# Hybrid layer step on Trainium2, SSD stage: the last places of groups 0 and 1 run behind the next group's first units; PSUM banks 4, 1, 3 instead of 3, 2, 3

## Chip, cores and metric

The kernel runs on one core of one Trainium2 chip. The metric is the device time of one execution in microseconds (us), the median of several runs.

## What is computed

One decoder layer with three parallel branches on 512 prompt rows and 64 sample rows (8 sequences of 8 new rows each). Only branch B, the Mamba-2 SSD, is touched. Cut to it, the reference is:

```
proj = rmsnorm(x) @ w_in                      # z, xBC, dt are slices of proj
xbc  = silu(causal_conv(xBC, conv_state))     # 4 taps; the last 3 rows of xBC are returned as the new conv state
xs, B, C = split(xbc);  dt = softplus(dt + dt_bias);  a = -exp(a_log)
# per group of 4 heads, in 4 chunks of 128 prompt rows; h is 64 x 128 for each head
y_diag = (C B^T * decay) (dt x)               # within a chunk
state  = B^T (wdec dt x);  h = dec*h + state  # from chunk to chunk
y_off  = (C h_prev) * exp(a_cs)               # from the chunks before
y = y_diag + y_off + d_skip*x;  y = rmsnorm_group(y * silu(z)) * g;  h_b = y
out += sigmoid(merge) * (h_b @ w_proj_b)
```

The sample rows go the same way as one chunk of 8 rows for each sequence, with a start state h0 of each sequence that is loaded from memory (8 x 32 heads x 64 x 128), read by C and rewritten.

## The kernel before

**Stages.** The span's first 651 us are the SSD stage; the other branches and the output projection follow and are not touched. There are 8 groups g. Activations lie in on-chip memory with channels across the 128 partitions and 576 rows (512 prompt, 64 sample) in the free direction, in two halves of 288.

**Units.** The stage's projections are a list of jobs, and each job has two halves; a half is called a unit here. A unit is 24 products of 128x128 by 128x288 into one PSUM bank (`gemm_half`, L167; each weight is taken as a high and a low part, and so is the activation, which makes three products for each of 8 blocks). A job's `load` fetches weights (L130, on SyncE), its `prep` splits them (`whi` on ScalarE L98, `wlo` on VectorE L99), its `half` runs the unit and evicts it. Job kinds: `conv_job(g, ci)` for the x, B and C columns of a group with the convolution behind it (evicted on ScalarE L412/L416, taps on VectorE L426, result L430/L437), `z_job` (evicted by tanh L470 on ScalarE and L471 on VectorE), `proj_job` (two times 12 products in each unit, added into `m_sb` by VectorE L763) and `gate_job`. While group g is worked on, the convolutions of group g+1 run.

**Places.** Between the units stands the small work of the SSD recurrence. `steps(g)` lists it as twelve places, and a table (`PLACES`) says behind which unit of the group each place comes. TensorE's order is just the order in which this program is written (`tc.manual_schedule` for TensorE alone); the order on VectorE, ScalarE, GpSimd and SyncE comes from a scheduler. The steps that matter below:

- `chunk_a(g, c)`: three transposes into an `sps` bank (L511), from which VectorE makes `xdt` and `xdd` (L514, L517) and ScalarE `BT` (L519); then `chunk_cb` forms C B^T (L540) and VectorE multiplies the decays `e` with it (L541).
- `decays(g, c)`: loads `e` by a DMA on SyncE's queue (L496), adds the mask (VectorE L497), exponentials (ScalarE L499). There are three buffers for `e`.
- `yd`: products into a `yps` bank (L556) and their addition to `ysb` (VectorE L567). `yd(g, 4)` is that of the sample rows; `c_h0` (L682, evicted by ScalarE L686) also uses `yps`.
- `state` (L575, first chunk evicted by ScalarE L579), `state_out` (L588/L590), `y_off` (L600/L603), `y_smp` (L613), `gate_y` (L693 to L695), `norm_y` (L707 to L713).
- `h0_T`: transposes of the sample's start states (L652, evicted by ScalarE L654); `h0_new`: the new states (L661, scaled on ScalarE L666, added on VectorE L667).
- `conv_out(g)`: a transpose (L446) into an `sps` bank, a copy (ScalarE L448), and eight DMAs that ScalarE issues (L451, L452).

**Banks.** The eight PSUM banks are dealt out as three pools, L67: `acc` for the units, `yps` and `sps` for the small work. Each pool goes round its banks, and a new use waits until the bank's last one has been read: with three `sps` banks the fourth small step in a row waits for the first one's readers.

Of the kernel before, what the change touches and what calls it, by code (L numbers as in the profile page):

```python
# [14 lines left out]
PSUM = bass.MemoryType.PSUM  # L15
# [27 lines left out]
def tile_hybrid_step(  # L43
# [20 lines left out]
    bank = {}  # L64

    def banks(stack, acc, y, s):

        for k, n in (("acc", acc), ("yps", y), ("sps", s)):
            bank[k] = stack.enter_context(tc.tile_pool(name=f"ps_{k}{acc}", bufs=n, space=PSUM, reuse_waits="tile"))

    def acc_tile():
        return bank["acc"].tile([P, 512], F32, tag="acc", name="acc")
# [113 lines left out]
    xl = lambda k: hn_lo[:, k]  # L186

    with ExitStack() as stb:
        banks(stb, 3, 2, 3)
        ws["pool"] = stb.enter_context(tc.tile_pool(name="wb", bufs=2))  # L190
        pb = stb.enter_context(tc.tile_pool(name="pb", bufs=1))
        xbuf = mpool.tile([P, KD * T], F32, tag="m", name="xbuf")
# [26 lines left out]
        for tiles in ((0, 1, 2), (3, 4)):  # L219
            n = len(tiles)  # L220
# [11 lines left out]
            w = 3 * P if n == 3 else P + TS  # L232
            for k in range(KD):
# [4 lines left out]
                g = gcol[:, k:k + 1]  # L238
# [408 lines left out]
        def h0_T(g, j, f):  # L647

            d = st_[g]
            tp = s_tile()  # L650
            for b in range(4):
                PE.transpose(tp[:, b * P:(b + 1) * P], d["h0", j][:, 4 * f + b], ident)  # L652
            h0T = pb.tile([P, 4 * P], F32, tag="h0T", name="h0T", bufs=2)
            d["h0T", j, f] = h0T, S.copy(h0T, tp)  # L654

        def h0_new(g, j, f):

            d = st_[g]
            xst, btd = d["st", f]
            sps = s_tile()  # L660
            PE.matmul(sps, lhsT=xst[:, 2 * j:2 * j + 2].rearrange("p h d -> p (h d)"),  # L661
                      rhs=btd.rearrange("p b n -> p (b n)"), start=True, stop=True)
            h4 = d["h0", j][:, 4 * f:4 * f + 4]
            dl = d["ebc"][:, j, TP + 32 * f:TP + 32 * f + 32].rearrange("p (b t) -> p b t", t=LS)[:, :, LS - 1:LS]
            for b in range(4):
                S.activation(h4[:, b], h4[:, b], AF.Copy, scale=dl[:, b])  # L666
            V.tensor_tensor(h4, h4, sps.rearrange("p (b n) -> p b n", b=4), ALU.add)  # L667
            if f == 1:
                hd = 4 * g + 2 * j
                S.dma_start(out=ssm_s[0, :, hd:hd + 2].rearrange("b r d n -> (r d) b n"), in_=d["h0", j])  # L670
# [72 lines left out]
        def proj_job(r, p):  # L743

            k = {}

            def load():
                if p % 2 == 0:
                    gate_th["p", r, p // 2] = load_block(w_proj_b[0], r * 512, 4, [(p * 256, 512)])

            def prep():
                k["w"] = wsplit(gate_th["p", r, p // 2], 4, (p % 2) * 256, 256)

            def half(j):
                jj = 2 * p + j
                w = [t[:, :, j * P:(j + 1) * P] for t in k["w"]]
                for f in range(2):
                    ps, sl = gemm_half(w, 4, lambda i: hb[4 * r + i][:, 0], lambda i: hb[4 * r + i][:, 1], f)
                    dst = m_sb[:, jj, sl]
                    if r == 0:  # L760
                        S.copy(dst, ps)
                    else:
                        V.tensor_tensor(dst, dst, ps, ALU.add)  # L763
                    if r == 3:
                        V.scalar_tensor_tensor(dst, gate_th[jj][:, sl], 1.0, dst, ALU.add, ALU.mult)
                if r == 3:
                    S.dma_start(out=m_scr[:, jj], in_=m_sb[:, jj])
            return Job(load, prep, half)


        with tc.manual_schedule(engines={mybir.EngineType.PE}):
            def group_jobs(g):

                c = [conv_job(g + 1, ci) for ci in range(4)] if g + 1 < G else [gate_job(0), gate_job(1), gate_job(2), gate_job(3)]
                z = [z_job(g, 0), z_job(g, 1)]
                if g == 0:
                    return [z[0], *c, z[1]]
                if g == 1:
                    return [c[0], c[1], z[0], c[2], c[3], z[1]]
                p = [proj_job(g // 2 - 1, 2 * (g % 2) + i) for i in range(2)]  # L780
                a, b = (p, z) if g % 2 else (z, p)
                return [c[0], a[0], c[1], a[1], c[2], b[0], c[3], b[1]]

            def yd(g, *cs):
                y_add(g, cs, y_diag(g, cs))

            def steps(g):

                w = [[] for _ in range(12)]
                w[0] = [lambda: start_y(g), lambda: decays(g, 2), lambda: chunk_a(g, 1)]  # L790
                w[1] = [lambda: state(g, 0)]
                if g > 0:
                    w[1] += [lambda: y_smp(g - 1), lambda: gate_y(g - 1)]
                w[2] = [lambda: state(g, 1), lambda: chunk_a(g, 2)]
                w[3] = [lambda: y_off(g, 1), lambda: yd(g, 0, 1), lambda: decays(g, 3)]
                if g > 0:
                    w[3] += [lambda: norm_y(g - 1)]
                w[4] = [lambda: state(g, 2), lambda: chunk_a(g, 3), lambda: decays(g, 4)]
                w[5] = [lambda: y_off(g, 2), lambda: chunk_a(g, 4), lambda: h0_load(g, 0)]
                w[6] = [lambda: state(g, 3), lambda: chunk_t4(g), lambda: h0_load(g, 1)]  # L800
                w[7] = [lambda: y_off(g, 3), lambda: chunk_cb(g, 4)]
                w[8] = [lambda: yd(g, 2, 3), lambda: state_out(g), lambda: h0_T(g, 0, 0)]
                w[9] = [lambda: h0_T(g, 0, 1), lambda: h0_new(g, 0, 0), lambda: h0_new(g, 0, 1)]
                w[10] = [lambda: c_h0(g, 0), lambda: h0_T(g, 1, 0), lambda: h0_T(g, 1, 1)]
                w[11] = [lambda: h0_new(g, 1, 0), lambda: h0_new(g, 1, 1), lambda: c_h0(g, 1), lambda: yd(g, 4)]
                return w

            halves = [(j, h) for j in (conv_job(0, ci) for ci in range(4)) for h in range(2)]  # L810
            between = {}

            def put(u, *fs):
                between.setdefault(u, []).extend(fs)

            put(7, lambda: decays(0, 0), lambda: decays(0, 1))
            PLACES = {0: (2, 3, 4, 5, 6, 7, 8, 9, 10, 11, 12, 13), 1: (1, 3, 4, 5, 6, 7, 8, 9, 10, 11, 12, 13)}
            for g in range(G):
                u0 = len(halves)
                halves += [(j, h) for j in group_jobs(g) for h in range(2)]  # L820
                n = len(halves) - u0
                if g == 0:
                    put(u0 + 1, lambda: chunk_a(0, 0), lambda: conv_out(0))
                else:

                    between[u0 - 1] = between.get(u0 - 1, []) + [lambda g=g: chunk_a(g, 0)]
                w = steps(g)
                at = PLACES.get(g, (1, 2, 3, 5, 6, 7, 8, 9, 11, 12, 13, 14) if g == 2 else (0, 1, 2, 4, 5, 7, 8, 9, 10, 12, 13, 14))
                for i, a in enumerate(at):
                    put(u0 + a, *w[i])  # L830
                if g + 1 < G:
                    put(u0 + n - 3, lambda g=g: decays(g + 1, 0), lambda g=g: decays(g + 1, 1))
                    put(u0 + n - 1, lambda g=g: conv_out(g + 1))
            units = []
            for u, x in enumerate(halves):
                units += [x, (None, between.get(u, []))]
            tail = {0: [lambda: y_smp(G - 1), lambda: gate_y(G - 1)], 5: [lambda: norm_y(G - 1)]}
            for i, u in enumerate([(j, h) for j in (gate_job(jj) for jj in range(4, 8)) for h in range(2)]):
                units += [u, (None, tail.get(i, []))]
            units += [(j, h) for j in (proj_job(3, p) for p in range(4)) for h in range(2)]  # L840

            jobs = [u[0] for u in units if u[0] is not None and u[1] == 0]
            at = {id(j): i for i, j in enumerate(jobs)}
            jobs[0].load()
            jobs[0].prep()
            jobs[1].load()
            for j, h in units:
                if j is None:
                    for w_ in h:
                        w_()  # L850
                    continue
                i = at[id(j)]
                if h == 0:
                    if i + 2 < len(jobs):
                        jobs[i + 2].load()
                    if i + 1 < len(jobs):
                        jobs[i + 1].prep()
                j.half(h)
# [587 lines left out]
    for i in range(4):  # L1446
# [17 lines left out]
        n = len(pieces)  # L1464
# [44 lines left out]
```

## Time and profile before

| | |
|---|---|
| median of 3 runs | 1154.28 us (1149.95 to 1155.85) |
| profiled execution, its own time | 1156.32 us |
| span of the profiled execution | 1154.6 us, mean granted TensorE clock 0.985 |
| TensorE matmuls (PE) | 1106.8 us busy, 96% |
| VectorE (DVE) | 780.2 us busy, 68% |
| ScalarE (ACT) | 619.9 us busy, 54% |
| GpSimd (POOL) | 28.4 us busy, 2% |
| chain of work that ended last | PE 89%, DVE 4%, DMA 3%, ACT 2%, issue 1% |

PE is the TensorE matmul, PEld its weight load, SP is SyncE; ACTq and SPq are the sequencers that issue DMAs. Busy means that at least one instruction runs. The granted clock is a share of the full 2.4 GHz: 1.00 is 2.4 GHz, 0.50 is 1.2 GHz, and a value between them is a stretch that was partly at one and partly at the other. A row of the timeline gives start, duration, the instruction, and in brackets how long the engine had been idle before it and what released it.

### The profile page before, as it was taken

The numbers are of one execution on the slowest core, as the hardware profiler recorded it, in microseconds if no ns is written. First come the engines' busy times: TensorE is split into PE (matmuls) and PEld (weight loads), VectorE is DVE, ScalarE is ACT, GpSimd is POOL, SyncE is SP. The second block draws the span as 40 slices with busy tenths as digits, with TensorE's granted clock in tenths as the row PEclk, the third lists the DMA queues.
The fourth block names the chain that finished last, engine by engine and source line by source line (L and its number), as shares of the span: only waits on it lengthen the run. The fifth ranks groups of instructions, "written<-read, shape, count | busy, mean of one in ns | idle before, by whom it ended". The sixth has DMA issues, their size and how long they took to land.

```text
span 1154.6 us, 20412 instructions
## 1 busy us (share of the span) xinstructions
PE 1106.8 (96%) x8200; PEld 1030.4 (89%) x8200; DVE 780.2 (68%) x1444; ACT 619.9 (54%) x1291; POOL 28.4 (2%) x109
## 2 busy tenths in 40 slices
PE   5999898999999989999999999999999999999997
PEld 3989887899999989999999877899999999889776
DVE  5778495867788686687634654786975567775743
ACT  6457576676767667565554244343653236564521
POOL 1010000000000000000000000000000000000000
PEclk9999898999999999999999999999999999999999
DMA  6433433445253534525242525631363353465411
GB/s 171 121 88 111 122 107 89 126 142 146 84 154 97 151 92 132 146 71 168 66 145 95 189 73 165 192 110 39 109 209 113 118 185 105 121 183 195 152 47 73
DMA packets 160334, 144.38 MB, mean 125 GB/s; under 512 B 10152, under 2 KB 141264, under 8 KB 160240
## 3 DMA queue, kind: packets, MB, share of 16 engines
q1 hardware_dynamic: 137136, 125.60, 35.5%
q10 hardware_dynamic: 23104, 17.49, 4.8%
q8 instruction: 64, 1.05, 0.4%
q14 instruction: 30, 0.25, 0.1%
HBM read 123.61 MB, written 19.46 MB: 124 GB/s over the span
## 4 chain that ended last, share of the span: by engine, by line
PE 89%; DVE 4%; DMA 3%; ACT 2%; issue 1%; SPq 0%; ACTq 0%; DVEq 0%
PE acc L167 37%; PE acc L923 15%; PE acc L154 12%; PE acc L1053 4%; PE acc L1458 4%; DMA e<-a_scr 2%; PE acc L1118 2%; PE yps L556 2%; PE sps L652 1%; PE sps L511 1%; PE sps L575 1%; DVE cacc L426 1%; PE sps L600 1%; PE yps L682 1%; PE sps L540 1%
## 5 line engine op out<-in xcount | busy, mean ns | idle before, releaser
L167 PE MATMUL acc<-hn_hi,whi 128*128 128x288 f32 x896 | 275.4, 307 | 2.0 <-ACT thm L740 0.8
L167 PE MATMUL acc<-hn_hi,wlo 128*128 128x288 f32 x896 | 269.0, 300 | 2.6 <-DVE wlo L99 2.6
L167 PE MATMUL acc<-hn_lo,whi 128*128 128x288 f32 x896 | 269.0, 300 | 0.0
L167 PEld LDWEIGHTS acc<-hn_hi,whi 128*128 128x128 f32 x896 | 173.1, 193 | 3.5 <-ACT thm L740 1.0
L167 PEld LDWEIGHTS acc<-hn_hi,wlo 128*128 128x128 f32 x896 | 172.6, 193 | 3.1 <-DVE wlo L99 3.1
L167 PEld LDWEIGHTS acc<-hn_lo,whi 128*128 128x128 f32 x896 | 173.0, 193 | 0.3
L98 ACT CAST w<-wraw 128x1024 fp32r<-128x1024 f32 (+1 forms) x64 | 59.2, 942 | 103.4 <-PE acc L923 24.0
L167 PE MATMUL acc<-hb,whi 128*128 128x288 f32 x512 | 105.2, 301 | 4.5 <-DVE m_sb L763 4.5
L99 DVE TENSOR_TENSOR wlo<-wraw,whi 128x1024 fp32r<-128x1024 f32 x72 | 87.9, 1220 | 28.9 <-ACT whi L98 28.7
L98 ACT CAST whi<-wraw 128x1024 fp32r<-128x1024 f32 x72 | 75.6, 1050 | 46.1 <-PE acc L167 43.9
L99 DVE TENSOR_TENSOR w<-wraw,w 128x1024 fp32r<-128x1024 f32 x64 | 68.5, 1087 | 36.3 <-ACT w L98 36.0
L923 PE MATMUL acc<-hn_hi,w 128*128 128x288 f32 x512 | 89.5, 300 | 0.0
L167 PEld LDWEIGHTS acc<-hb,whi 128*128 128x128 f32 x512 | 82.0, 189 | 5.2 <-DVE m_sb L763 5.0
L923 PE MATMUL acc<-tT,w 128*128 128x288 f32 x576 | 85.9, 298 | 0.0
L426 DVE SCALAR_TENSOR_TENSOR cacc<-raw,cwh,cacc 128x600 f32<-128x600 f32 x96 | 80.5, 839 | 7.3 <-ACT cacc L424 6.6
L923 PEld LDWEIGHTS acc<-tT,w 128*128 128x128 f32 x576 | 78.4, 188 | 0.9 <-issue 0.9
L923 PEld LDWEIGHTS acc<-hn_hi,w 128*128 128x128 f32 x512 | 74.1, 188 | 2.1 <-DVE thx L941 0.5
L167 PE MATMUL acc<-hb,wlo 128*128 128x288 f32 x256 | 75.7, 296 | 0.0
L99 DVE TENSOR_TENSOR w<-S,w 128x1024 fp32r<-128x1024 f32 x32 | 39.2, 1224 | 25.0 <-ACT w L98 25.0
L499 ACT ACTIVATE e<-e,nacs 128x128 f32<-128x128 f32 (+1 forms) x160 | 49.7, 381 | 8.7 <-DVE e L497 8.7
L154 PE MATMUL acc<-ha,w 128*128 128x288 f32 x384 | 51.6, 295 | 0.0
L154 PE MATMUL acc<-hn_hi,w 128*128 128x288 f32 x256 | 51.2, 295 | 0.0
(393 smaller groups left out, 2122.5 us busy)
## 6 DMA issues: line engine op xcount, KB each, us to landing
wraw<-in_w_in_dram SPq DMA_DIRECT2D x44, 1024.0 KB
wraw<-in_w_in_dram SPq DMA_DIRECT2D x16, 512.0 KB
e<-a_scr SPq DMA_DIRECT2D x32, 256.0 KB
h<-in_state_ssm_dram SPq DMA_DIRECT2D x16, 512.0 KB
out_dram<-h ACTq DMA_DIRECT2D x16, 512.0 KB
wraw<-in_w_proj_b_dram SPq DMA_DIRECT2D x8, 1024.0 KB
ebc<-e_scr SPq DMA_DIRECT2D x16, 288.0 KB
wraw<-in_w_mem_kv_dram SPq DMA_DIRECT2D x4, 1024.0 KB
```

What stands on the lines that cost most here:

```text
L98: S.copy(hi, v)
L99: (e or V).tensor_tensor(lo, v, hi, ALU.subtract)
L154: PE.matmul(ps[:n, :width], lhsT=a, rhs=b[:, sl], start=(i == 0), stop=(i == last))
L167: PE.matmul(ps[:, 0:HT], lhsT=a[:, k], rhs=b(k)[:, sl], start=(n == 0), stop=(n == 3 * nk - 1))
L426: V.scalar_tensor_tensor(a[:, 0:n], raw[:, i:i + n], cwh[:, i, q:q + 1], a[:, 0:n], ALU.mult, ALU.add)
L499: S.activation(e[:, h, 0:w], e[:, h, 0:w], AF.Exp, bias=nacs[:, c, h0_ + h:h0_ + h + 1])
L511: PE.transpose(tp[:, j * P:(j + 1) * P], xs[:, j, c0:c0 + P], ident)
L556: m = PE.matmul(y4[64 * r:64 * r + 64, i, j], lhsT=xdt[:, h], rhs=e[:, h, 0:w], start=True, stop=True)
L923: PE.matmul(ps[:, 0:HT], lhsT=w[:, r, k], rhs=x(q, k), start=first and n == 0, stop=n == 11, skip_group_check=True)
L1053: PE.matmul(pss[i], lhsT=x(k)[:, c], rhs=w[:, r, k2], start=(k + q == 0), stop=(k == KD - 1 and q == 2))
L1118: PE.matmul(pss[i], lhsT=x[xr], rhs=w[:, r, k2], start=(k + q == 0), stop=(k == KD - 1 and q == 2))
L1458: PE.matmul(ps[:, 0:cn], lhsT=x(k)[:, c], rhs=w, start=(k + q == 0), stop=(k == KD - 1 and q == 2))
```

## The change

Five edits, all in the order of the SSD stage or in its banks. The number of instructions on each engine stays as it is.

1. Banks: `acc` 4, `yps` 1, `sps` 3 instead of 3, 2, 3 (the pool's name is made from another number so that it stays unique).
2. Group 0's places come one unit later, so that its last one falls behind the third unit of group 1; group 1's last three places come one unit later. `chunk_a(0, 0)` and `conv_out(0)` too come one unit later; `chunk_a(1, 0)` and `chunk_a(2, 0)` stay behind the last unit of the group before.
3. Group 2's jobs stand in another order (c0 c1 z0 z1 c2 p0 c3 p1 instead of c0 z0 c1 z1 c2 p0 c3 p1), and its places follow the table that group 1 had before.
4. `yd(g, 4)`, the sample's in-chunk products, moves in all groups from the end of the last place (w[11], behind `c_h0(g, 1)`) to the start of place 9 (w[9]), two places earlier.
5. `conv_out(1)` and `conv_out(2)` move from the last unit of the group before to a place behind the fourth unit of their own group, ahead of `state(g, 0)`, `y_smp` and `gate_y` there. The others stay.

```diff
-            bank[k] = stack.enter_context(tc.tile_pool(name=f"ps_{k}{acc}", bufs=n, space=PSUM, reuse_waits="tile"))
+            bank[k] = stack.enter_context(tc.tile_pool(name=f"ps_{k}{y}", bufs=n, space=PSUM, reuse_waits="tile"))
...
-        banks(stb, 3, 2, 3)
+        banks(stb, 4, 1, 3)
...
+                if g == 2:
+                    return [c[0], c[1], z[0], z[1], c[2], proj_job(0, 0), c[3], proj_job(0, 1)]
...
-                w[9] = [lambda: h0_T(g, 0, 1), lambda: h0_new(g, 0, 0), lambda: h0_new(g, 0, 1)]
+                w[9] = [lambda: yd(g, 4), lambda: h0_T(g, 0, 1), lambda: h0_new(g, 0, 0), lambda: h0_new(g, 0, 1)]
                 w[10] = [lambda: c_h0(g, 0), lambda: h0_T(g, 1, 0), lambda: h0_T(g, 1, 1)]
-                w[11] = [lambda: h0_new(g, 1, 0), lambda: h0_new(g, 1, 1), lambda: c_h0(g, 1), lambda: yd(g, 4)]
+                w[11] = [lambda: h0_new(g, 1, 0), lambda: h0_new(g, 1, 1), lambda: c_h0(g, 1)]
...
-            PLACES = {0: (2, 3, 4, 5, 6, 7, 8, 9, 10, 11, 12, 13), 1: (1, 3, 4, 5, 6, 7, 8, 9, 10, 11, 12, 13)}
+            PLACES = {0: (3, 4, 5, 6, 7, 8, 9, 10, 11, 12, 13, 14), 1: (1, 3, 4, 5, 6, 7, 8, 9, 10, 12, 13, 14),
+                      2: (1, 3, 4, 5, 6, 7, 8, 9, 10, 11, 12, 13)}
...
-                    put(u0 + 1, lambda: chunk_a(0, 0), lambda: conv_out(0))
+                    put(u0 + 2, lambda: chunk_a(0, 0), lambda: conv_out(0))
...
-                    put(u0 + n - 1, lambda g=g: conv_out(g + 1))
+                    put(u0 + n + (3 if g < 2 else -1), lambda g=g: conv_out(g + 1))
```

**TensorE, where group 0 ends and group 1 begins.** `sps` and `yps` are tiles of those pools, `h` the start states, `xs`, `B` and `C` the convolved columns; "x4" counts instructions. Before, in a row:

```order
L652 MATMUL sps<-ident,h_1194 128x128 x4
L661 MATMUL sps<-btd,xst 128x512 x2
L446 MATMUL sps<-ident,cg 108x128
L511 MATMUL sps<-ident,xs 128x128 x3
L540 MATMUL sps<-C,xs 128x128
```

These five steps take six `sps` banks one after the other with no unit between them. With the change, in a row:

```order
L556 MATMUL yps<-e,xdt 64x128 x8
L588 MATMUL sps<-ident,hT 128x128 x2
L652 MATMUL sps<-ident,h_1229 128x128 x4
L511 MATMUL sps<-ident,xs 128x128 x3
L540 MATMUL sps<-C,xs 128x128
```

The first steps of the next group (L511, L540) now follow the end of `yd` and the first `h0_T` (L652), one unit ahead of the second `h0_T`, and the two L661 and `conv_out`'s L446 have gone to later units.

**ScalarE, in the first units of group 1**, around the copy of the first chunk's state, L579. Before:

```order
L98 CAST whi<-wraw 128x1024
L416 COPY raw<-acc 128x224
L417 COPY raw<-acc 128x8x8
L579 COPY hT<-sps 128x256
L424 ACTIVATE cacc<-raw,cbh,cwh 128x600
L470 ACTIVATE th<-acc 128x288
L694 ACTIVATE zs<-ysb 128x1152
```

With the change:

```order
L452 DMA out_dram<-co 24x128
L428 ACTIVATE raw<-cacc 128x600
L451 DMA out_dram<-co 3x128
L452 DMA out_dram<-co 24x128
L579 COPY hT<-sps 128x256
L694 ACTIVATE zs<-ysb 128x1152
L470 ACTIVATE th<-acc 128x288
```

The last of the eight DMA issues of `conv_out` now stand ahead of L579 on ScalarE, and so does the tanh of the convolution (L428).

**VectorE, at the end of group 3**, where only `yd(3, 4)` has moved; L567 with 128x2x64 is its addition, and L497 the masks of the next group's decays. Before:

```order
L99 TENSOR_TENSOR wlo<-wraw,whi 128x1024
L667 TENSOR_TENSOR h_3547<-h_3547,sps 128x512 x2
L420 COPY cg<-raw 128x3
L421 COPY cg<-raw 128x24
L426 SCALAR_TENSOR_TENSOR cacc<-raw,cwh,cacc 128x600 x3
L99 TENSOR_TENSOR wlo<-wraw,whi 128x1024
L430 SCALAR_TENSOR_TENSOR C<-raw,cacc 128x512
L434 SCALAR_TENSOR_TENSOR C<-raw,cacc 128x64
L471 SCALAR_TENSOR_TENSOR zs<-th,acc 128x288
L667 TENSOR_TENSOR h_3604<-h_3604,sps 128x512 x2
L567 TENSOR_TENSOR ysb<-ysb,yps 128x2x64
L497 TENSOR_TENSOR e<-e,tri 128x512
```

With the change:

```order
L497 TENSOR_TENSOR e<-e,tri 128x512 x2
L471 SCALAR_TENSOR_TENSOR zs<-th,acc 128x288
L99 TENSOR_TENSOR wlo<-wraw,whi 128x1024
L567 TENSOR_TENSOR ysb<-ysb,yps 128x2x64
L667 TENSOR_TENSOR h_3547<-h_3547,sps 128x512 x2
L420 COPY cg<-raw 128x3
L421 COPY cg<-raw 128x24
L497 TENSOR_TENSOR e<-e,tri 128x512
L426 SCALAR_TENSOR_TENSOR cacc<-raw,cwh,cacc 128x600 x3
```

The addition L567 now stands ahead of the first two L667, and the third mask L497 ahead of the convolution's taps L426.

## Rows read from the trace of the kernel before

**Rows 1.** Busy time by stretch. Columns: the stretch in us from the span's start, its length, busy us (and count) of PE, PEld, DVE, ACT and POOL, the granted TensorE clock, the DMA engines' busy share, GB/s.

```profile
71.00:77.00 6.00, 6.00 (x36) 6.00 (x36) 1.46 (x4) 0.67 (x2) 0.25 (x2) 0.72 0.70 184
...
116.00:124.00 8.00, 6.72 (x29) 6.35 (x30) 4.22 (x7) 3.48 (x10) 0.00 (x0) 0.57 0.43 119
...
133.00:138.00 5.00, 5.00 (x27) 5.00 (x28) 5.00 (x9) 2.71 (x7) 0.68 (x1) 0.66 0.39 114
...
181.00:189.00 8.00, 7.27 (x34) 6.55 (x37) 3.08 (x5) 2.98 (x9) 0.00 (x0) 0.57 0.28 76
...
198.00:203.00 5.00, 5.00 (x27) 4.92 (x26) 4.95 (x9) 2.56 (x8) 1.06 (x1) 0.66 0.37 105
...
260.00:405.00 145.00, 144.25 (x1174) 139.56 (x1174) 111.23 (x218) 99.50 (x236) 4.24 (x22) 1.00 0.44 127
...
426.00:431.00 5.00, 4.27 (x21) 4.27 (x22) 4.51 (x11) 3.59 (x8) 0.48 (x3) 0.66 0.01 2
```

**Rows 2.** The timeline of PE: the matmuls from 67 to 430 us before which it had waited (one of 0.75 at 359.01 stands in rows 7), with what released them.

```profile
70.80 0.49 PE L540 MATMUL sps<-C,xs 128*128 128x128 f32 x2 [2.58 <-DVE C L430]
...
116.71 0.46 PE L446 MATMUL sps<-ident,cg 128*108 128x128 f32 x1 [2.39 <-ACT h0T L654]
...
117.73 0.90 PE L511 MATMUL sps<-ident,xs 128*128 128x128 f32 x3 [0.57 <-DVE h L667]
...
132.96 0.46 PE L540 MATMUL sps<-C,xs 128*128 128x128 f32 x2 [1.96 <-DVE h L667]
...
152.56 0.40 PE L167 MATMUL acc<-hn_hi,whi 128*128 128x288 f32 x1 [0.76 <-DVE zs L471]
...
161.67 0.52 PE L511 MATMUL sps<-ident,xs 128*128 128x128 f32 x3 [0.80 <-ACT BT L519]
...
180.84 0.32 PE L446 MATMUL sps<-ident,cg 128*108 128x128 f32 x1 [1.78 <-DVE h L667]
...
181.47 0.90 PE L511 MATMUL sps<-ident,xs 128*128 128x128 f32 x3 [0.30 <-ACT h0T L654]
...
182.80 0.79 PE L540 MATMUL sps<-C,xs 128*128 128x128 f32 x2 [0.43 <-ACT co L448]
...
197.59 0.46 PE L540 MATMUL sps<-C,xs 128*128 128x128 f32 x2 [1.96 <-DVE h L667]
...
211.45 0.40 PE L167 MATMUL acc<-hn_hi,whi 128*128 128x288 f32 x1 [0.49 <-ACT raw L412]
...
226.92 0.52 PE L511 MATMUL sps<-ident,xs 128*128 128x128 f32 x3 [1.91 <-issue]
...
407.82 0.53 PE L167 MATMUL acc<-hb,whi 128*128 128x288 f32 x2 [1.78 <-DVE m_sb L763]
...
426.73 0.53 PE L167 MATMUL acc<-hb,whi 128*128 128x288 f32 x2 [2.76 <-DVE m_sb L763]
```

**Rows 3.** The timeline of PE at the end of group 0, the small steps alone (24 matmuls of L167 stand between 109.61 and 113.26).

```profile
108.31 1.09 PE L556 MATMUL yps<-e,xdt 128*64 128x128 f32 x16
...
109.61 0.60 PE L652 MATMUL sps<-ident,h 128*128 128x128 f32 x4
...
113.26 0.60 PE L652 MATMUL sps<-ident,h 128*128 128x128 f32 x4
...
113.61 0.71 PE L661 MATMUL sps<-btd,xst 96*128 96x512 f32 x2
```

**Rows 4.** The timeline of SyncE's queue, VectorE and ScalarE around the decays of groups 1 and 2.

```profile
109.01 0.92 SPq L496 DMA_DIRECT2D e<-a_scr  x2
...
112.72 1.49 DVE L497 TENSOR_TENSOR e<-e,tri 128x512 f32<-128x512 f32 x2 [0.91 <-DMA e<-a_scr]
113.44 2.45 ACT L499 ACTIVATE e<-e,nacs 128x128 f32<-128x128 f32 x8 [0.89 <-DVE e L497]
...
179.01 0.69 DVE L430 SCALAR_TENSOR_TENSOR C<-raw,cacc 128x512 f32<-128x512 f32 x1
```

**Rows 5.** The timeline of ScalarE and its queue: the first issue of `conv_out(1)`, the first and last of `conv_out(3)`, each with the copy that follows the eight, and the copy L579 of group 1.

```profile
119.37 0.41 ACTq L451 DMA_DIRECT2D out_dram<-co  x1
...
123.24 0.27 ACT L519 COPY BT<-sps 128x128 f32<-128x128 f32 x1 [4.02 <-DMA out_dram<-co]
...
142.52 0.39 ACT L579 COPY hT<-sps 128x256 f32<-128x256 f32 x1
...
260.89 0.27 ACTq L451 DMA_DIRECT2D out_dram<-co  x1
...
263.72 0.27 ACT L519 COPY BT<-sps 128x128 f32<-128x128 f32 x1 [1.91 <-DMA out_dram<-co]
```

**Rows 6.** The timeline at the end of group 3: the decays' DMA, its mask, the first L667 behind it, and `c_h0(3, 0)` on PE.

```profile
304.29 0.91 SPq L496 DMA_DIRECT2D e<-a_scr  x2
...
311.05 0.69 DVE L497 TENSOR_TENSOR e<-e,tri 128x512 f32<-128x512 f32 x1 [2.48 <-DMA e<-a_scr]
...
314.01 0.68 DVE L667 TENSOR_TENSOR h<-h,sps 128x512 f32<-128x512 f32 x1
...
315.90 0.64 PE L682 MATMUL yps<-h0T,C 128*32 128x128 f32 x16
```

**Rows 7.** The timeline of PE: the two units of groups 4 and 6 whose weights come late.

```profile
359.01 0.40 PE L167 MATMUL acc<-hn_hi,wlo 128*128 128x288 f32 x1 [0.75 <-DVE wlo L99]
...
498.54 0.40 PE L167 MATMUL acc<-hn_hi,wlo 128*128 128x288 f32 x1 [1.86 <-DVE wlo L99]
```

More of the change, by code (lines that the diff above doesn't have):

```diff
@@ L827, in tile_hybrid_step @@
                 w = steps(g)
-                at = PLACES.get(g, (1, 2, 3, 5, 6, 7, 8, 9, 11, 12, 13, 14) if g == 2 else (0, 1, 2, 4, 5, 7, 8, 9, 10, 12, 13, 14))
+                at = PLACES.get(g, (0, 1, 2, 4, 5, 7, 8, 9, 10, 12, 13, 14))
                 for i, a in enumerate(at):
```

## The prediction, made before the changed kernel was timed

> **What bounds the kernel now.** TensorE does: the chain of work that ended last is PE for 89%, so a microsecond is won only where PE idles or runs below full clock. I first read the busy time by stretch, for the places where the clock falls. From 260 to 405 us PE is busy for 144.25 of 145 us at a granted clock of 1.00: there is nothing to win. Around 71, 116, 133, 181, 198 and 426 us the clock falls to 0.57 to 0.72 of 2.4 GHz [rows 1]; each of these stretches begins with a wait of PE. Then I read PE's waits in the timeline [rows 2]. They lie where one group ends and the next begins (116 to 133 and 180 to 198 us), at the first C B^T of group 0 (70.8), at three waits of 0.5 to 1.9 in groups 1 and 2, and at two projection units of group 5 that wait for an `acc` bank (407.8, 426.7). A stretch costs its length times the share of clock that it lacks: 1.7 us for 71 to 77, 3.4 for each of the two of 8 us, 1.7 for each of the three of 5 us.
>
> **What the change removes.** Each term is the idle time [rows 2] plus the clock [rows 1].
> - a. C B^T of group 0 waits 2.58 for `C` from VectorE (70.80). It comes one unit later; a unit is 3.2 us (from the L652 at 109.61 to that at 113.26 it is 3.65, of which 0.35 is the four transposes, as from 113.26 to 113.61) [rows 3]. So the wait is covered: 2.6 + 1.7 = 4.3.
> - b. End of group 0: six small steps in a row want six `sps` banks of three (116.71 and 117.73). `conv_out(1)` leaves, and `chunk_a(1, 0)` now stands one unit ahead of the rest: 2.39 + 0.57 + 3.4 = 6.4.
> - c. C B^T at 132.96 waits for both L667 of the same place. They move one unit behind it: 1.96 + 1.7 = 3.7.
> - d. The same at the end of group 1 (180.84, 181.47, 182.80): 1.78 + 0.30 + 0.43 + 3.4 = 5.9.
> - e. 197.59, as c: 3.7.
> - f. Two units wait for an `acc` bank, 0.76 at 152.56 and 0.49 at 211.45. A fourth bank gives each eviction one unit more, 3.2 us: 1.25.
> - g. 226.92, 1.91 put down to "issue": the transposes wait for the read of `BT`, which on ScalarE stands behind two casts and a copy. In the new job order it stands directly behind the casts of `hb`: 1.9. The 0.80 at 161.67 stays.
> - h. 407.82 and 426.73 wait 1.78 and 2.76 for `m_sb` on VectorE. Here a fourth bank gives half a unit (12 products), 1.6 us for each, and then the next unit wants the bank of the same row. I take 1.6 twice, and the lowered clock of 426 to 431: 4.9.
>
> Sum: 32.0 us.
>
> **Fourth `acc` bank, row against rule.** In f and h the rows name the reader of the bank as the releaser, so banks limit there: with them the sum holds 6.1 us for it. The Trainium skill, "TensorE: Matmul & The Clock Gate", section "HAM oscillation — how this bites in real kernels", reports a kernel in which more PSUM buffering gave no further gain (125.5 against 126.6 us). By that rule the sum here would be 25.9. I stay with the rows, because that kernel is said to wait for DMAs, and the waits in f and h end with VectorE and ScalarE.
>
> **What it adds or uncovers.** No instruction is added. The new order has its own waits, none of which the trace shows, so each is worked out from rows and bounded.
> - At `h0_new` of group 0, PE wants the bank of `chunk_a(1, 0)`, which is free when ScalarE has copied `BT`. That copy stands behind the eight exponentials, these behind the masks, these behind the DMA, which is issued at 109.01 when `yd` has read the old `e`: mask from 112.72 to 114.21, exponentials from 113.44 to 115.89 [rows 4], copy 0.27 [rows 5], so 116.2. PE gets there at 109.61 + 3.65 [rows 3] + about 1.2 for `chunk_a`, `yd(0, 4)` and a transpose step = 114.5. Wait 1.8 (bounds 0 and 2.96, the sum of the old waits at b).
> - C B^T of `chunk_a(1, 1)` now stands directly behind the second `h0_T`, and VectorE's second L667 behind the mask of the third `e`, whose DMA goes out when `yd(0, 4)` is done: 3.7 from issue to mask [rows 4], then 0.7 and 0.7, 5.1 in all, against some 5.5 on PE. Nearly even: 1.0 (bounds 0 and 1.96, the row at c). The same place in group 1: 0.9.
> - C B^T of `chunk_a(2, 0)` needs `C` of group 2, ready at 179.70 [rows 4]; PE came to L446 at 180.84 - 1.78 = 179.06 [rows 2], behind a transpose step and the two L661 (0.35 and 0.71 [rows 3]), which now come later; with 0.3 for its own transposes it is there at 178.3: 1.4 (0 to 2.58).
> - `conv_out(1)` and `conv_out(2)` now stand ahead of L579 on ScalarE, which in group 1 ran at 142.52. Eight issues took 3.9 (119.37 to 123.24) and 2.8 (260.89 to 263.72) [rows 5]. With the tanh among them, L579 is some 5 us behind the transpose, and its bank is wanted again after some 4 (a unit and two steps): 1.0 and 1.2, 2.2 in all (bounds 0, and 2 times 2.8). What is behind L579, the square of `gate_y` and the tanh of a unit, waits with it; the fourth `acc` bank covers that.
> - In groups 3 and later only `yd(g, 4)` moves. It frees the third `e` buffer two units sooner, its DMA passes the `h0` load or a weight load on SyncE's queue, and in group 5 two masks stand ahead of the products for `hb`. There a unit's `wlo` may come late, as in groups 4 and 6 (0.75 and 1.86 [rows 7]): I take the middle, 1.3 (0 to 1.86). Those two stay.
> - One of these may lower the clock, as some waits of this size did and some did not [rows 1, 2]: one times 1.7.
>
> Sum of the new: 1.8 + 1.0 + 0.9 + 1.4 + 2.2 + 1.3 + 1.7 = 10.3.
>
> **One `yps` bank** I cost at nothing. The five uses in a group now stand at least one unit apart, `yd(g, 4)` no longer directly behind `c_h0(g, 1)`. The cover is that unit: an addition or copy must be done 3.2 us after its products. It is thinnest in group 3, where the masks' DMA took 6.8 us from issue to mask; L567 takes the place that L667 had at 314.01, and the next user of the bank is at 315.90 [rows 6]. With 0.3 for the addition 1.6 us are left.
>
> **Net:** 32.0 - 10.3 = 21.7 us. The profiled execution took 1156.3 us, so it would take 1134.6. The median of the runs shown is 2.0 below it: 1132.6 us.
>
> **Rivals.**
> 1. Slower: the single `yps` bank becomes the bound. VectorE takes its work in order, and L567 of `yd(g, 4)` stands behind two masks that wait for a DMA. If these come over 1.6 us later than at 311.05 [rows 6], or L567 as late in the other groups, `c_h0(g, 0)` waits in each of the 8 groups. At the price of c (1.96 and 1.7 of clock) that is 8 times 3.7 = 29: 1162. For it: no spare bank is left. Against it: the masks of group 1 came 3.7 us after the issue [rows 4], and PE would have to pass each group's point with under 1.6 us lost elsewhere. Chance 0.06. The Trainium skill speaks for this rival: "Perfetto Trace Analysis", section "Matmuls", wants independent groups of products to rotate through different PSUM banks so that one's eviction overlaps the next; here the unit between does that, and no row of this trace has a one-bank pool.
> 2. Partly: the group ends keep stalls. The four waits at b, c, d and e come back at 1.96 and 1.7 each, 14.6 instead of 5.1 + 1.7: the gain is 13.9, 1140.4. If the fourth `acc` bank gives nothing besides, 7.8: 1146.5. For it: like idle times in rows 2 stand with a lowered clock (1.96 at 132.96) and without one (1.91 at 226.92). Chance 0.21.
> 3. No change: as 2 with both losses, and `conv_out` ahead of L579 costs a whole run of issues and a lowered clock each time, 2 times (2.8 + 1.7) = 9.0 instead of 2.2. The gain is 1.0: 1153. For it: the eight issues already delayed a `BT` copy by 4.0 and 1.9 [rows 5]. Against it: PE did not wait there. Chance 0.10.
>
> **The numbers.** My forecast has 0.63, of which its own bounds take in 1121 (no new wait at all, and h whole) to 1140. A measurement can tell about 0.5% from no change, 5.8 us: faster is below 1148.5, slower above 1160.1. Faster: 0.63 + 0.21 = 0.84; same 0.10; slower 0.06. The range is 1122 to 1147: it takes in the forecast and rival 2, and leaves out rivals 1 and 3 and a little below.
>
> **What would show it.** Right: no stretch of lowered clock at 71 to 77; at most one between the ends of groups 0 and 2, where there were four; no wait for L763; group 3 and 4 as before. Waits of 1 to 2 us for `BT` L519 at an L661, for `h0T` or L667 at an L540, for `C` L430 at an L540 of group 2. Wrong: PE's L682 or L556 waiting for L567 or L686 (rival 1); an L511 waiting over 2 us for L579 with the clock down (rival 3); `acc` waits as before (the rule). The stage after 651 us must keep its length; if it doesn't, the difference there is none of this.

## The result, and the profile after

The changed kernel took 1134.2 us (median of 4 runs, 1132.22 to 1134.75), the kernel before 1153.47 (4 runs, 1149.95 to 1155.85): ratio 0.9847, 95% interval 0.9822 to 0.9872 (the ratio on record is not the quotient of the two medians, which is 0.9833 and lies inside the interval). The forecast was 1132.6 (1122 to 1147). The profiled execution took 1134.07 us, its span fell from 1154.6 to 1132.3 us, 22.3 less; the forecast for that was 21.7.

Busy time by stretch of the changed kernel, the places of [rows 1] (they come earlier now; 136 to 144 for the third, 476 to 484 for the late unit of group 6) and two more, columns as there:

```profile
44.00:50.00 6.00, 6.00 (x43) 5.82 (x43) 4.25 (x12) 3.48 (x6) 0.44 (x3) 0.72 0.40 105
70.00:76.00 6.00, 6.00 (x49) 6.00 (x48) 3.62 (x7) 1.74 (x5) 0.25 (x2) 1.00 0.66 176
116.00:122.00 6.00, 5.36 (x26) 5.15 (x26) 2.75 (x5) 3.72 (x13) 0.00 (x0) 0.72 0.39 101
136.00:144.00 8.00, 6.24 (x54) 5.67 (x55) 7.97 (x17) 4.70 (x8) 0.62 (x3) 1.00 0.51 136
180.00:188.00 8.00, 6.95 (x66) 6.10 (x62) 6.83 (x13) 7.41 (x21) 0.49 (x3) 1.00 0.67 196
198.00:203.00 5.00, 5.00 (x27) 5.00 (x28) 4.55 (x9) 2.89 (x5) 0.61 (x3) 0.66 0.17 35
262.00:396.00 134.00, 133.08 (x1084) 127.77 (x1083) 103.27 (x202) 93.04 (x219) 5.00 (x23) 1.00 0.45 127
408.00:413.00 5.00, 4.89 (x39) 4.68 (x38) 5.00 (x9) 3.17 (x5) 0.00 (x0) 1.00 0.01 3
476.00:484.00 8.00, 7.32 (x56) 6.98 (x55) 7.88 (x17) 5.35 (x15) 0.48 (x3) 1.00 0.02 4
629.00:1132.00 503.00, 492.50 (x3383) 444.39 (x3383) 324.85 (x543) 218.90 (x362) 1.29 (x1) 1.00 0.40 129
```

Of the six stretches with a lowered clock of [rows 1] four are gone; 116 to 122 and 198 to 203 are left, at 1.7 us each, and one of that price is new at 44 to 50 us, ahead of every step that the change moves; PE had waited nowhere from 30 us on, and in the kernel before these 6 us ran at 1.00. The kernel before had a seventh lowered stretch, which [rows 1] leave out, behind the late weights of 498.54 [rows 7]; it too is gone:

```profile
498.00:504.00 6.00, 5.46 (x29) 5.34 (x30) 5.54 (x13) 3.76 (x11) 0.48 (x3) 0.72 0.01 4
```

What follows the SSD stage kept its length: 501.8 us before and 501.7 after, from the first matmul behind it to the end.

The timeline of PE, the matmuls before which it waited in the SSD stage, all of them; these answer to [rows 2, 7]:

```profile
116.64 0.73 PE L661 MATMUL sps<-btd,xst 96*128 96x512 f32 x2 [1.54 <-DVE e L541]
124.40 0.49 PE L540 MATMUL sps<-C,xs 128*128 128x128 f32 x2 [0.40 <-ACT h0T L654]
139.19 0.49 PE L540 MATMUL sps<-C,xs 128*128 128x128 f32 x2 [1.76 <-ACT hT L579]
153.11 0.52 PE L511 MATMUL sps<-ident,xs 128*128 128x128 f32 x3 [0.25 <-ACT BT L519]
171.25 0.49 PE L540 MATMUL sps<-C,xs 128*128 128x128 f32 x2 [1.30 <-DVE C L430]
182.52 0.49 PE L540 MATMUL sps<-C,xs 128*128 128x128 f32 x2 [1.05 <-ACT h0T L654]
197.90 0.49 PE L540 MATMUL sps<-C,xs 128*128 128x128 f32 x2 [2.39 <-ACT hT L579]
345.94 0.40 PE L167 MATMUL acc<-hn_hi,wlo 128*128 128x288 f32 x1 [0.84 <-DVE wlo L99]
478.13 0.40 PE L167 MATMUL acc<-hn_hi,wlo 128*128 128x288 f32 x1 [0.68 <-DVE wlo L99]
```

Every wait that the prediction wanted gone is gone, and nearly all that are left stand at steps that it named (the 0.25 at 153.11 is the old 0.80 at 161.67): h0_new of group 0 (1.54, forecast 1.8, though the row names VectorE's L541 where the prediction had the copy `BT`), C B^T behind `h0_T` (0.40 and 1.05; 1.0 and 0.9), `C` of group 2 (1.30; 1.4), L579 (1.76 and 2.39; 1.0 and 1.2). PE's waits in the stage sum to 10.2 us in these rows against 23.9 before.

A second profiled execution of the same kernel (e0 below) has the same span, 1132.3, but other numbers. From its waits of PE between 60 and 640 us (total, times, longest):

```profile
PE sps L540 <- ACT hT L579: 3.3, 2, 2.0
PE acc L167 <- DVE wlo L99: 3.0, 2, 1.9
PE sps L540 <- ACT h0T L654: 2.7, 2, 1.6
PE yps L1067 <- issue: 1.7, 1, 1.7
PE sps L511 <- DVE h L667: 1.6, 2, 1.2
PE sps L540 <- DVE C L430: 1.3, 1, 1.3
PE sps L661 <- DVE e L541: 0.7, 1, 0.7
PE sps L511 <- ACT BT L519: 0.7, 1, 0.7
PE acc L167 <- DVE m_sb L763: 0.3, 1, 0.3
```

Without L1067, which is no longer in this stage, they sum to 13.6, 3.4 more, and nowhere in the stage is the clock lowered. So a single wait is known to about a microsecond. Sums agree better, but only with the clock in them: waits and what the lowered clock costs make 18.0 us in the first execution and 15.9 in the second, at one span.

### The profile page after: what moved, and what is told of

It reads as the page before. It is cut to its first block, busy times and chain, and to the rows that moved or that the text cites. A ratio compares the mean times of both kernels' runs of the same rounds, so it can differ in the third digit from the quotient of the medians.

```text
span 1132.3 us, 20429 instructions
## 1 busy us (share of the span) xinstructions
PE 1099.1 (97%) x8200; PEld 1022.9 (90%) x8200; DVE 781.2 (69%) x1444; ACT 618.5 (55%) x1291; POOL 25.3 (2%) x109
## 3 DMA queue, kind: packets, MB, share of 16 engines
q8 instruction: 64, 1.05, 0.4%
## 4 chain that ended last, share of the span: by engine, by line
PE 88%; DMA 4%; DVE 3%; ACT 2%; issue 1%; SPq 0%; ACTq 0%; DVEq 0%
PE acc L167 35%; PE acc L926 16%; PE acc L154 12%; PE acc L1056 4%; PE acc L1461 4%; DMA e<-a_scr 3%; PE acc L1121 2%; PE yps L556 2%; PE sps L575 1%; PE sps L652 1%; PE sps L511 1%; PE sps L600 1%; PE sps L540 1%; DVE cacc L426 1%; PE yps L1409 1%
## 5 line engine op out<-in xcount | busy, mean ns | idle before, releaser
L167 PE MATMUL acc<-hn_hi,whi 128*128 128x288 f32 x896 | 272.3, 304 | 0.1
L167 PE MATMUL acc<-hn_hi,wlo 128*128 128x288 f32 x896 | 266.5, 297 | 1.5 <-DVE wlo L99 1.5
L167 PE MATMUL acc<-hn_lo,whi 128*128 128x288 f32 x896 | 266.4, 297 | 0.0
L167 PEld LDWEIGHTS acc<-hn_hi,whi 128*128 128x128 f32 x896 | 170.4, 190 | 1.9 <-issue 1.5
L167 PEld LDWEIGHTS acc<-hn_hi,wlo 128*128 128x128 f32 x896 | 170.1, 190 | 2.0 <-DVE wlo L99 2.0
L167 PEld LDWEIGHTS acc<-hn_lo,whi 128*128 128x128 f32 x896 | 170.5, 190 | 0.4
L167 PE MATMUL acc<-hb,whi 128*128 128x288 f32 x512 | 104.5, 299 | 0.1
L426 DVE SCALAR_TENSOR_TENSOR cacc<-raw,cwh,cacc 128x600 f32<-128x600 f32 x96 | 80.4, 838 | 4.7 <-ACT cacc L424 4.0
L167 PEld LDWEIGHTS acc<-hb,whi 128*128 128x128 f32 x512 | 81.6, 188 | 1.0 <-issue 0.6
L167 PE MATMUL acc<-hb,wlo 128*128 128x288 f32 x256 | 75.3, 294 | 0.0
```

The lines of the kernel that those rows point to most:

```text
L167: PE.matmul(ps[:, 0:HT], lhsT=a[:, k], rhs=b(k)[:, sl], start=(n == 0), stop=(n == 3 * nk - 1))
L426: V.scalar_tensor_tensor(a[:, 0:n], raw[:, i:i + n], cwh[:, i, q:q + 1], a[:, 0:n], ALU.mult, ALU.add)
```

## The experiments

"Waits" is the sum of PE's waits in the SSD stage (60 to 640 us, without L1067) in the profiled execution, "clock" the mean granted clock of its span.

| run | median us (range, n) | ratio to before, 95% | waits | clock |
|---|---|---|---|---|
| before | 1153.47 (1149.95 to 1155.85, 4) | 1 | 23.9 | 0.985 |
| changed | 1134.2 (1132.22 to 1134.75, 4) | 0.9847 (0.9822 to 0.9872) | 10.1 | 0.993 |
| e0_changed_again | 1134.77 (1134.0 to 1137.21, 4) | 0.9837 (0.9805 to 0.9869) | 13.6 | 0.998 |
| e1_banks323 | 1138.4 (1133.02 to 1139.73, 6) | 0.9855 (0.9817 to 0.9893) | 14.0 | 0.993 |
| e2_old_order_banks413 | 1158.74 (1156.33 to 1162.99, 10) | 1.0061 (1.0034 to 1.0088) | 29.7 | 0.983 |
| e3_conv_out_back | 1132.64 (1131.13 to 1137.29, 6) | 0.9826 (0.9792 to 0.9859) | 11.1 | 0.999 |
| e4_conv_out_late | 1139.19 (1138.05 to 1143.79, 6) | 0.9881 (0.9848 to 0.9915) | 15.8 | 0.994 |
| e5_group2_order_back | 1134.81 (1133.36 to 1136.81, 5) | 0.9834 (0.9806 to 0.9863) | 11.6 | 0.999 |
| e6_banks_and_yd4_only | 1148.79 (1146.43 to 1154.17, 12) | 0.9965 (0.9944 to 0.9986) | 19.3 | 0.991 |
| e7_order_only | 1144.52 (1141.0 to 1149.85, 12) | 0.9938 (0.9917 to 0.9959) | 18.5 | 0.990 |
| e10_conv_out_one_later | 1133.69 (1132.04 to 1135.41, 6) | 0.9823 (0.9794 to 0.9852) | 12.6 | 0.998 |
| e12_own_e_buffer | 1130.41 (1128.65 to 1132.81, 6) | 0.9813 (0.9786 to 0.9840) | 8.2 | 0.997 |
| e13_e12_banks323 | 1129.48 (1128.64 to 1131.33, 5) | 0.9793 (0.9773 to 0.9813) | 10.1 | 0.998 |
| e14_e12_conv_out_as_changed | 1131.65 (1130.1 to 1134.33, 4) | 0.9809 (0.9786 to 0.9832) | 9.0 | 0.998 |

The kernel before had medians of 1151.9 to 1154.5 beside them. Differences below are of medians; where the ratios say something else, that stands beside it.

**e1_banks323**

```diff
-        banks(stb, 4, 1, 3)
+        banks(stb, 3, 2, 3)
```

> The changed kernel's order with the old banks (acc 3, yps 2, sps 3). If three acc banks limited f and h, their waits return: a unit waits 0.5 to 0.8 for an acc bank once or twice, two projection units wait 1.6 to 2.8 for m_sb L763, one of them with a lowered clock; 6.1 us more than the changed kernel, 1140 (1138 to 1143). If a fourth acc bank gives nothing, 1134 and no wait of L167 for L763. If one yps bank had cost something, under 1134.

1138.4, 4.2 more, but the two intervals overlap, and by the ratios it is 0.9. Its six runs go from 1133.0 to 1139.7 us: the two fastest had a mean clock of 0.997 and 0.998, the four others 0.993 to 0.995. The waits for L471 and L412 of term f did not come back: here the new order had removed them by itself. One wait for L763 did, with a lowered clock behind it; from the timeline of PE and the busy time by stretch:

```profile
410.11 0.53 PE L167 MATMUL acc<-hb,whi 128*128 128x288 f32 x2 [2.66 <-DVE m_sb L763]
```

```profile
410.00:416.00 6.00, 5.89 (x33) 5.89 (x34) 5.67 (x13) 4.50 (x8) 0.49 (x3) 0.72 0.00 1
```

**e2_old_order_banks413**

```diff
-        banks(stb, 3, 2, 3)
+        banks(stb, 4, 1, 3)
```

(in the kernel before)

> The order of before with the new banks (acc 4, yps 1, sps 3), nothing else. My theory is that one yps bank is free only because the change puts a unit between its uses: here yd(g, 4) stands directly behind c_h0(g, 1), so PE's L556 waits for the copy L686 in each of the 8 groups, 0.5 to 2.8 us by how late ScalarE is, with a lowered clock (1.7) in some; 8 times about 2.5 = 20 more, less the 6.1 of the fourth acc bank: about 1167 (1155 to 1180). If one bank is free in any order: 1153.5 - 6.1 = 1147.

1158.74, slower than before, if less than expected. From the waits of PE between 60 and 640 us:

```profile
PE yps L556 <- ACT yos L686: 14.5, 8, 2.7
```

One wait in each of the 8 groups, as expected: two uses of the one `yps` bank stand next to each other. So one bank costs time where two uses stand next to each other. In the changed kernel, with a unit between them, no PE wait names L567 or L686.

**e3_conv_out_back**

```diff
-                    put(u0 + n + (3 if g < 2 else -1), lambda g=g: conv_out(g + 1))
+                    put(u0 + n - 1, lambda g=g: conv_out(g + 1))
```

> The changed kernel with conv_out(1) and conv_out(2) back at the last unit of the group before, ahead of chunk_a. The two waits of L540 for hT L579 (1.76 and 2.39, and 1.7 of clock) go, 5.9 less; but the transpose takes an sps bank in a row of five, and the issues stand among the exponentials ahead of the copy BT, so h0_new waits longer, 2 to 4 us for each and with the clock down: about 1137 (1133 to 1143). If it doesn't matter where ScalarE issues these DMAs, 1134 with the waits of L540 for L579 unchanged.

1132.64, under both forecasts and not told from the changed kernel. Both waits for L579 are gone, and the copy `BT` comes late at h0_new, but by less than I had feared and at full clock; from the timeline of PE:

```profile
117.35 0.50 PE L661 MATMUL sps<-btd,xst 96*128 96x512 f32 x1 [1.79 <-ACT BT L519]
```

**e4_conv_out_late** (`u0 + n + (8 if g < 2 else -1)`)

> The changed kernel with conv_out(1) and conv_out(2) five units later, behind the ninth unit of their own group, far from L579. If the eight issues and the tanh ahead of L579 make PE wait, both waits of L540 for hT L579 go and the lowered clock at 199 with them: 1134.2 - 5.9 = 1128.3 (1126 to 1131). If the wait only moves with the issues to the step that stands behind them there, or if L579 is late for another reason, 1133 to 1136.

1139.19, above both forecasts: the wait moved, as the rival has it, and grew. The eight issues now stand ahead of ScalarE's evictions of the last convolution of group 2, and `C` comes late; from ScalarE's and then PE's timeline:

```profile
165.24 0.26 ACT L635 CAST bst<-sps 96x128 fp32r<-96x128 f32 x1 [4.84 <-DMA out_dram<-co]
165.41 0.34 ACT L416 COPY raw<-acc 128x224 f32<-128x224 f32 x1
```

```profile
175.19 0.80 PE L540 MATMUL sps<-C,xs 128*128 128x128 f32 x2 [4.30 <-DVE C L430]
```

In the changed kernel L416 of that unit ran at 160.93 and the wait for `C` was 1.30.

**e10_conv_out_one_later** (`u0 + n + (4 if g < 2 else -1)`)

Why L579 is late in the changed kernel was first read from ScalarE's timeline in group 1:

```profile
135.72 0.31 ACTq L452 DMA_DIRECT2D out_dram<-co  x1
137.61 0.70 ACT L428 ACTIVATE raw<-cacc 128x600 f32<-128x600 f32 x1 [2.81 <-DVE cacc L426]
138.12 0.25 ACTq L451 DMA_DIRECT2D out_dram<-co  x1
138.41 0.31 ACTq L452 DMA_DIRECT2D out_dram<-co  x1
138.76 0.37 ACT L579 COPY hT<-sps 128x256 f32<-128x256 f32 x1 [0.45 <-DMA out_dram<-co]
```

Six issues were done at 136.0; then ScalarE waited at the tanh L428 until 137.6 for VectorE's taps, with L579 queued behind it.

> The changed kernel with conv_out(1) and conv_out(2) one unit later, behind state(g, 0), y_smp and gate_y, so that on ScalarE L579 stands ahead of the tanh L428 and of all eight issues. If L579 is late in the changed kernel because it stands behind L428, which waits for VectorE's taps, both waits of L540 for L579 go (1.76, 2.39 and 1.7 of clock): 1134.2 - 5.9 = 1128.3, or up to 1132 if BT L519 behind the issues makes a later step wait. If the wait moves in full to that step: 1134 or more.

1133.69, not told from 1134.2. The waits for L579 went, as the theory has it, but others of the same sum came: PE now waits 1.92 for `hT` L582, 1.3 for `BT` and 0.7 for `co`, and 12.6 in all. The expected 5.9 is refuted.

The cause, too, holds for group 1 alone. In group 2, where PE's wait was the larger one (2.39), ScalarE's timeline in the changed kernel is another:

```profile
192.99 0.37 ACTq L452 DMA_DIRECT2D out_dram<-co  x1
196.18 0.25 ACTq L451 DMA_DIRECT2D out_dram<-co  x1
...
196.88 0.70 ACT L428 ACTIVATE raw<-cacc 128x600 f32<-128x600 f32 x1 [4.79 <-DMA out_dram<-co]
197.49 0.35 ACT L579 COPY hT<-sps 128x256 f32<-128x256 f32 x1
```

Here all eight issues, from 191.30 to 196.78, stand ahead of the tanh. Between the sixth and the seventh lies a pause of 2.8 us in which ScalarE ran nothing. VectorE's taps were done at 195.9, before the seventh. What ends the pause no run shows.

**e5_group2_order_back** (the line `if g == 2` taken out, group 2's places `(1, 2, 3, 5, 6, 7, 8, 9, 11, 12, 13, 14)`)

> The changed kernel with group 2's old job order and its old places. If the new order is what put the copy BT directly behind the casts of hb, L511 waits 1.9 for it again at about 215, and the rest is as in the changed kernel: 1136 (1134.5 to 1139). If that wait went away for another reason (the fourth acc bank, the other times of the group), 1134 and no such wait.

1134.81, the changed kernel's own time beside it being 1134.77. The wait came back as forecast; from the timeline of PE:

```profile
209.49 0.52 PE L511 MATMUL sps<-ident,xs 128*128 128x128 f32 x3 [1.91 <-issue]
```

So the cause of term g is right and its worth is not: the wait is back and the time is the same.

**e6_banks_and_yd4_only** (before, with `banks(stb, 4, 1, 3)` and `yd(g, 4)` at the start of w[9])

> The order of before with two of the five edits: banks 4, 1, 3, and yd(g, 4) at place 9. The waits of L556 for L686 that the new banks alone brought go (with them it took 1159), and the terms f and h stay won: 1153.5 - 6.1 = 1147.4 (1145 to 1150), with the six waits at the group ends and the one at 70.8 as in the kernel before. If a fourth acc bank gives nothing, 1153; if the yd(g, 4) place alone doesn't cure the one bank, over 1155 with waits for L567 or L686.

1148.79, 4.9 less than the 1153.69 beside it. No wait for L686 is left, and that for L763 fell from 4.5 to 0.3 us.

**e7_order_only** (changed, with banks 3, 2, 3 and `yd(g, 4)` at the end of w[11])

> The other part of the change: places, group 2's order and conv_out as changed, but banks 3, 2, 3 and yd(g, 4) at its old place. If the two parts add up, the banks with yd(g, 4) gave 4.9 (1148.8 against 1153.7), the whole change 19, and this gives the other 14: about 1139.5 (1137 to 1142), with the waits for L763 and their lowered clock in group 5. If the parts need each other, it is over 1144: group ends in which yd(g, 4) at its old place makes the first steps of the next group wait again.

1144.52, 7.4 less than the 1151.94 beside it: the parts need each other. 4.9 and 7.4 make 12.3 of the 19 (by the ratios 11.2 of 17.6). Against e1_banks323 only `yd(g, 4)` differs, and that is 6.1 us (9.6 by the ratios), with intervals that do not meet. ScalarE and SyncE's queue in group 1 (SyncE first), and PE:

```profile
126.49 0.37 SPq L496 DMA_DIRECT2D e<-a_scr  x1
```

```profile
130.71 1.28 ACT L499 ACTIVATE e<-e,nacs 128x128 f32<-128x128 f32 x4
...
137.96 0.37 ACT L579 COPY hT<-sps 128x256 f32<-128x256 f32 x1 [4.64 <-DMA out_dram<-co]
```

```profile
138.39 0.80 PE L540 MATMUL sps<-C,xs 128*128 128x128 f32 x2 [3.63 <-ACT hT L579]
```

The third decays' DMA waits for the `e` buffer that `yd(g, 4)` reads. At its old place it goes out at 126.49 and its four exponentials run at 130.71, among the evictions and issues ahead of L579. In e1_banks323 it goes out at 115.05, and PE waits less (SyncE's queue, then PE):

```profile
115.05 0.37 SPq L496 DMA_DIRECT2D e<-a_scr  x1
```

```profile
137.63 0.49 PE L540 MATMUL sps<-C,xs 128*128 128x128 f32 x2 [1.28 <-ACT hT L579]
```

L579 follows its matmul by 8.2 us here (129.80 to 137.96) and by 5.9 in e1 (131.36 to 137.21). About half of the 2.3 us between them lies ahead of the copy `co`, where the exponentials stand; the other half lies in the eight issues, which take 5.4 us and not 4.2. PE's two waits for L579 are 7.2 us against 3.5 in e1; the rest of the 6.1 is not broken down.

**e12_own_e_buffer**

```diff
-            e = d["ex", c] = pb.tile([P, 4, P], F32, tag="e", name="e", bufs=3)
+            e = d["ex", c] = pb.tile([P, 4, w], F32, tag="e4" if smp else "e", name="e", bufs=1 if smp else 3)
...
-            co = pb.tile([108, P], F32, tag="co", name="co", bufs=1)
+            co = pb.tile([108, P], F32, tag="bst", name="co", bufs=2)
```

(and `conv_out` as in e3_conv_out_back)

> conv_out back as in e3_conv_out_back, and the sample's decays in an e buffer of their own (a fourth, half as wide; the copy co shares the buffers of bst to make room). The first decays of the next group then load when yd(g, 0, 1) is done, and not both behind yd(g, 2, 3), so four of the eight exponentials and a mask leave the chain that ends in the copy BT. If that chain (DMA, masks, exponentials, BT) is what PE waits for at h0_new of group 0 and at C B^T behind it, 2 to 5 us less than e3_conv_out_back: 1129.5 (1127 to 1131.5). If what is left are other waits of the same size, 1132 to 1135.

1130.41, 2.2 less than e3_conv_out_back and its median under every run of the changed kernel; the ratios' intervals overlap. The first decays of group 1 now load, get their mask and most of their exponentials before `yd(0, 2, 3)`; from SyncE's queue, VectorE and ScalarE:

```profile
89.87 0.46 SPq L496 DMA_DIRECT2D e<-a_scr  x1
```

```profile
102.32 0.68 DVE L497 TENSOR_TENSOR e<-e,tri 128x512 f32<-128x512 f32 x1
```

```profile
105.75 0.98 ACT L499 ACTIVATE e<-e,nacs 128x128 f32<-128x128 f32 x3
```

PE waits 0.9 at h0_new instead of 1.8, and 8.2 in all, the least of all runs.

**e14_e12_conv_out_as_changed** (e12 with `conv_out` where the change puts it)

> e12_own_e_buffer with conv_out(1) and conv_out(2) where the change puts them, so that against the changed kernel only the e buffers (and the place of co) differ. If the own buffer alone shortens the chain of DMA, masks, exponentials and BT: 1131.5 (1129 to 1133), the wait of L661 for L541 (1.5 and 0.7 in two runs of the changed kernel) under 1, and the waits of L540 for L579 as in the changed kernel. If the 4 us came from conv_out's place, 1134.

1131.65, as forecast, and the wait of L661 is gone. That the own buffer brings most of the gain is what the medians point to; the intervals of this run, of e12 and of the changed kernel overlap.

**e13_e12_banks323** (e12 with banks 3, 2, 3)

> e12_own_e_buffer with banks 3, 2, 3: the worth of the fourth acc bank once more, in the kernel with the fewest other waits, since e1_banks323 against the changed kernel (1138.4 against 1134.2) left it inside the two intervals. If the bank is worth the 4 to 6 us of terms f and h: 1135.5 (1133.5 to 1138), with PE waiting for L763 in group 5 for 1.6 us or more and the clock down there. If it is worth nothing: 1130 to 1132.

1129.48, no more than with the fourth `acc` bank; the 4 to 6 us lie outside the two intervals. Yet the waits for such a bank are there; from the waits of PE, and the stretch around the first:

```profile
PE acc L167 <- DVE m_sb L763: 3.0, 1, 3.0
...
PE acc L167 <- DVE zs L471: 1.5, 2, 0.8
...
PE acc L167 <- ACT thm L740: 0.8, 1, 0.8
```

```profile
399.00:408.00 9.00, 6.02 (x47) 5.79 (x46) 9.00 (x19) 4.32 (x10) 0.00 (x0) 1.00 0.01 3
```

They make 5.3 us of 10.1; in e12, which has none of them, other waits and one lowered clock (1.7 us at 44 to 52, before any of these steps) make up for it in the profiled execution.

**e0_changed_again** is the changed kernel beside e5, e6 and e10.

> The changed kernel itself, for comparison beside these on the same chip: 1134 (1132 to 1137).

## Why the prediction was right, and which steps were not

- **The total.** Right, 1.6 us from the median and 0.5 from the profiled execution (1134.6 forecast, 1134.07 measured): most of the 1.6 is the 2.0 that I took off for the median, which the changed kernel's median does not show. It was made as a sum of waits and lowered clock, and that sum holds to 1 to 3 us: waits fell by 13.8, and the clock's loss, span times what the mean lacks to 1, from 17.3 (0.015 of 1154.6) to 7.9 (0.007 of 1132.3). 23.2 in all, and the span fell by 22.3; in e0 the same sum is 25.3 for the same span. That it came so close is in part luck. My terms make 9.7 of waits (18.3 removed, 8.6 new) and 11.9 of clock (13.6 and 1.7), so the waits were 4.1 too small and the clock 2.5 too large. And the lowered stretch at 498 us that I had not listed went, while one came at 44 us, 1.7 each.
- **a to e, the group ends.** Right in place, and near in size: their old waits and all but two lowered clocks are gone, and e6_banks_and_yd4_only, which keeps the old places, has the waits still. The sign "at most one" lowered stretch there failed in this execution (two, at 116 and 198) and held in e0 (none). Of the new waits at these steps 4.3 came for 5.1 forecast. At h0_new PE was released by VectorE's L541, done at 116.59; the copy `BT` that I had named was done at 116.78. Both stand behind the masks and exponentials of the chain that I added up (whose terms make 1.7, not 1.8).
- **conv_out ahead of L579.** Right in place; 4.2 and 1.7 of clock in one execution, 3.3 and none in the other, for 2.2. Mis-sized: I took 2.8 to 3.9 us for the eight issues. In group 2 they took 5.5, with a pause of 2.8; there the wait was 2.39 with the clock down, the size that rival 3 gives one place (2.8 and 1.7). In group 1 six were done in 2 us, and the rest was the tanh behind VectorE's taps, queued ahead of L579. And the price is not one of the place: e3, e10 and the change itself are not told apart.
- **f and h, the fourth `acc` bank.** The step that failed: 6.1 us for it. Beside an old order it and the moved `yd(g, 4)` bring 4.9 (e6). In the new order it brings 4.2 by the medians and 0.9 by the ratios, inside the intervals (e1), and nothing in e13. The rows named the bank rightly, and one wait of h came back in e1 with its lowered clock (2.66 and 1.7); but f's waits went by the new order alone there (in e13 two of 0.8 for L471 are back). That a wait for VectorE that goes only brings PE sooner to the next thing that VectorE makes is how I read e12 beside e13; no run isolates it. The rule that I had put aside, of the Trainium skill, "TensorE: Matmul & The Clock Gate", section "HAM oscillation — how this bites in real kernels", agrees with e13 in its outcome. The kernel it is told of waits for DMAs; the waits here end with VectorE and ScalarE.
- **g.** The cause is right; no gain is seen (e5).
- **yd(g, 4).** I costed its place at nothing but for late weights. That step was wrong: with the later places of groups 0 and 1 it is worth 6.1 (e7 against e1, both with the old banks). By the traces 3.7 of that are the two waits for L579: its place sets when an `e` buffer is free, and so when four exponentials take ScalarE's time. The forecast hid this, since it took the whole change at once.
- **Late weights.** I had "those two stay", and 1.3 more in group 5. The changed kernel has 0.84 and 0.68 at full clock; e0 has 1.9 as the longest. That differs between executions of one kernel, and why is left open.
- **One `yps` bank.** Right: no wait. In group 3, the thinnest cover, L567 ended at 300.1 and the next user came at 302.56, 2.4 us for the 1.6 forecast. Two uses next to each other do cost time: e2 shows 14.5 us of it, through L686 on ScalarE. The first rival's own case, a late L567, no run shows. For that place the Trainium skill, "Perfetto Trace Analysis", section "Matmuls", which wants uses rotated through banks, agrees with e2; with a unit between them, the changed kernel shows no loss.

The lowest median is that of e13, 1129.5 us: the changed order, an own `e` buffer for the sample's decays, `conv_out` at its old place, and the old banks. e12 and e14 are not told from it.

## To carry to other kernels

Moving work apart so that no bank is wanted twice within one unit paid here; adding a bank where a row names one may not, as e13 shows. Cost a moved step by everything that it frees: here a buffer, whose refill started four exponentials on another engine. Where an engine carries waits of its own, such as a tanh behind another engine's taps or a run of DMA issues with a pause in it, what counts is which of them stands ahead of the instruction that PE needs.

## What the runs showed of the hardware

- The clock does not follow the length of one wait. In e13 PE waited 3.0 us and the granted clock of the stretch stayed at 1.00; in the changed kernel it fell to 0.72 behind 1.54 us and stayed at 1.00 around 1.76, and at 44 to 50 us it fell to 0.72 with PE busy for 6.00 of 6.00 and no wait since 30 us. Two executions of the changed kernel differ in that (0.993 and 0.998 of full clock over the span) at the same span.
- ScalarE's DMA issues hold back its own instructions: a run of eight, with a pause of 2.5 us ahead of the last, left it without a computation for 4.84 us (e4). Eight such issues took 2.8 us without a pause ([rows 5], `conv_out(3)`) and 5.5 with one (changed kernel, group 2).
